# A two-layer decoder trunk on one core: where the seven-product sums are combined, which rings the short weight chunks use, and how far the up projection runs ahead

## The chip, the cores and the metric

One core of one Trainium2 chip. The metric is the device time of one execution in microseconds (us), the median of the runs shown. The engines are called by their names in the profile: PE (TensorE), DVE (VectorE), ACT (ScalarE), POOL (GpSimd), SP (SyncE, which issues the weight loads).

## The reference

The kernel computes two residual layers on x of 256 positions by 2048 channels, all in float32, and a last RMSNorm. Each layer has a mixer (attention of several kinds, with an input and an output projection) and an MLP:

```
for layer in range(DEPTH):                 # DEPTH = 2
    h = rms_norm(x, attn_norm[layer])
    x = x + mixer(h)                       # even: MLA and MoBA, odd: dilated and sliding window
    h = rms_norm(x, mlp_norm[layer])
    x = x + jnp.square(jax.nn.relu(h @ w_up[layer])) @ w_down[layer]
return rms_norm(x, final_norm)
```

`w_up[layer]` is 2048 x 8192 and `w_down[layer]` 8192 x 2048. The change touches the MLPs, the way in which all weights are split, and where the gain of the last norm is loaded.

## The kernel before, in words

**Numbers.** A product in float32 is made of three passes on PE: each operand is split into a `hi` and a `lo` half, and hi\*hi, hi\*lo and lo\*hi are summed in PSUM. ACT makes `hi` (line 1276, a copy that rounds), DVE makes `lo` (line 1284, the difference).

**Weights and the stream.** All weights come in units of up to 1 MB (tile `raw`, three buffers, loaded by SP) and are used in chunks of up to 1024 columns. One list, `stream`, has all chunks in the order in which PE uses them; the main loop walks it. Before chunk i it makes `hi` up to chunk i + 4 and `lo` up to chunk i + 3 (`hi_to(i + HI_BUFS)`, `lo_to(i + LO_BUFS)`, rings of 5 and 4 slots of 1024 columns). When the `lo` of a unit's last chunk is made, the unit's buffer is free, and the next unit's load is issued. Each engine executes its instructions in the order in which this loop writes them.

**The MLP.** The 8192 hidden channels are cut into eight groups of 1024. A group's up projection (`up_list`, kind "U", 16 chunks) gives `up` banks, and `up_done` applies relu and the square. Groups 0 to 6, the plain groups, go down by a scheme of seven products in place of eight (Strassen's, in Winograd's form): `product_list` has, for each of four column blocks `cb` of 512 output columns, eight chunks of kind "S"; one in four, `single`, is only 512 columns wide. DVE prepares the sums of weight blocks (`prep13`, `prep24`, tiles `w13` and `w24`). The seven products of a column block stand in the PSUM banks `s0` and `s1`; `products_done` copies them to `stage` (ACT) and adds them to `sums` in DRAM with an accumulating DMA of POOL (line 1077). In the stream two product chunks of group g stand before each up chunk of group g + 1. Group 7 goes down directly, at the end of the MLP (kind "T", and "last" for the last block of the second MLP): eight blocks of 256 output columns, two chunks each; `down_done` evacuates a block, scales it and adds it to `xT`.

**The combine.** In group 6, when a column block's second bank is done, `products_done` starts a job `combine(cb)`: it reads the sums of that column block from DRAM (line 1085, tile `s` of the ring `hs`), DVE adds the seven products to four results (lines 1090 to 1095), ACT scales them (line 1098), PE transposes them in two halves (line 1105), and DVE adds each half to `xT` (line 1106). When both the combine and the direct part of a block are done, `finish` starts what follows: in the first MLP `make_xs` (the next mixer's input, lines 233 and 234, and a sum of squares, 241 to 245), in the second `final_block` (transposes and products with the gain, line 1197), at the end `last_block`.

**Jobs.** A job is a Python generator that writes its next instructions at a tick; `yield d, pe` puts its next step d ticks later. There is a tick after each second product chunk, after each up chunk and after each chunk of the direct down projection. The main loop writes a chunk's matmuls first, then the tick's.

## Time and profile before

| what | value |
|---|---|
| median of three runs | 2223.31 us (2222.3 to 2231.39) |
| the profiled execution, its own time | 2223.32 us |
| its span, first to last instruction | 2221.5 us |
| mean granted clock of PE | 0.987 of 2.4 GHz |
| PE busy | 2156.0 us, 97% |
| PE weight loads busy | 2058.3 us, 93% |
| DVE busy | 1745.0 us, 79% |
| ACT busy | 1316.7 us, 59% |
| POOL busy | 108.9 us, 5% |
| moved by DMA | 455.51 MB, mean 205 GB/s |

The shares are means over stages. The page's slices show PE at nine tenths or more nearly everywhere, and less in a few slices near 1000 us and after 2050 us. A wait of PE counts there; idle time of another engine counts only if PE waits for it.

### The profile page before, as it was taken

What the parts mean: (1) busy time and instruction counts of PE and PEld (TensorE: products, weight loads), DVE (VectorE), ACT (ScalarE), POOL (GpSimd) and SP (SyncE); (2) the same over time, 40 slices, a digit from 0 to 9 for tenths busy, and PEclk for the clock granted to TensorE, in tenths of its full rate; (3) what the DMA queues carried; (4) which work ended last, traced back from release to release, by engine and by line L of the source; (5) the groups of instructions that cost most, each with busy time, mean ns of one, the idle gap of its engine ahead of it and who ended that gap; (6) DMA issues with size and microseconds to landing.
All of it is one profiled execution on the core that took longest, in us unless ns stands there. A gap on an engine that the chain in (4) does not pass through costs nothing.

```text
span 2221.5 us, 39419 instructions
## 1 busy us (share of the span) xinstructions
PE 2156.0 (97%) x16086; PEld 2058.3 (93%) x16086; DVE 1745.0 (79%) x2248; ACT 1316.7 (59%) x1777; POOL 108.9 (5%) x144
## 2 busy tenths in 40 slices
PE   9999999999999999978999999999999999999787
PEld 7898989999999999978888899899999999999776
DVE  6765666898999999977966665568898999999766
ACT  6554545566667666655655446455666666666553
POOL 0000000000000000000000000000000000000000
PEclk9999999999999999999999999999999999999898
DMA  8545456577888888877554456565778888888772
GB/s 264 171 148 161 152 188 177 183 248 216 239 229 246 232 240 240 238 218 227 175 171 136 154 185 191 147 191 179 250 223 241 229 242 235 240 239 233 210 230 83
DMA packets 297685, 455.51 MB, mean 205 GB/s; under 512 B 10696, under 2 KB 172560, under 8 KB 297376
## 3 DMA queue, kind: packets, MB, share of 16 engines
q1 hardware_dynamic: 280224, 392.32, 56.0%
q0 software_dynamic: 17248, 60.67, 13.0%
q8 instruction: 126, 2.06, 0.4%
q14 instruction: 55, 0.45, 0.1%
q10 hardware_dynamic: 32, 0.01, 0.0%
HBM read 399.49 MB, written 53.48 MB: 204 GB/s over the span
## 4 chain that ended last, share of the span: by engine, by line
issue 26%; PE 20%; DMA 2%; POOL 2%; DVE 2%; ACT 1%; POOLq 0%; ACTq 0%; DVEq 0%; SPq 0%
PE mm L472 7%; PE mm L473 4%; POOL sums L1077 2%; PE mm L457 1%; PE mm L458 1%; PE mm L459 1%; DMA sums<-stage 1%; DMA hs<-sums 1%; PE up L463 1%; PE up L464 1%; PE up L465 1%; DVE lo L1284 1%; PE side L350 1%; DMA raw<-w_up 1%; PE mm L475 1%
## 5 line engine op out<-in xcount | busy, mean ns | idle before, releaser
L1284 DVE TENSOR_TENSOR lo<-raw,hi 128x1024 fp32r<-128x1024 f32 (+1 forms) x756 | 825.1, 1113 | 189.2 <-PE mm L473 74.9
L1276 ACT ACTIVATE hi<-raw 128x1024 fp32r<-128x1024 f32 (+1 forms) x756 | 717.9, 966 | 413.8 <-DMA raw<-w_up 169.2
L465 PE MATMUL up<-xs,lo 128*128 128x256 f32 x2048 | 579.6, 283 | 6.6 <-DVE lo L1284 6.2
L463 PE MATMUL up<-xs,hi 128*128 128x256 f32 x2048 | 578.8, 283 | 1.6 <-DVE xT L757 1.6
L464 PE MATMUL up<-xs,hi 128*128 128x256 f32 x2048 | 579.0, 283 | 0.0
L496 PE MATMUL s<-hi,hs 128*128 128x256 f32 x1568 | 445.7, 284 | 0.0
L497 PE MATMUL s<-lo,hs 128*128 128x256 f32 x1568 | 444.1, 283 | 0.0
L498 PE MATMUL s<-hi,hs 128*128 128x256 f32 x1568 | 443.7, 283 | 0.0
L465 PEld LDWEIGHTS up<-xs,lo 128*128 128x128 f32 x2048 | 387.8, 189 | 12.0 <-DVE lo L1284 11.2
L463 PEld LDWEIGHTS up<-xs,hi 128*128 128x128 f32 x2048 | 385.2, 188 | 1.9 <-ACT hi L1276 1.9
L464 PEld LDWEIGHTS up<-xs,hi 128*128 128x128 f32 x2048 | 385.0, 188 | 0.0
L472 PE MATMUL mm<-xs,hi 128*128 128x512 f32 x885 | 319.5, 401 | 0.4 <-ACT hi L1276 0.4
L1276 ACT ACTIVATE hi<-w 128x1024 fp32r<-128x1024 f32 x224 | 236.1, 1054 | 130.3 <-DVE w L1050 85.6
L496 PEld LDWEIGHTS s<-hi,hs 128*128 128x128 f32 x1568 | 300.1, 191 | 0.0
L497 PEld LDWEIGHTS s<-lo,hs 128*128 128x128 f32 x1568 | 300.1, 191 | 0.0
L498 PEld LDWEIGHTS s<-hi,hs 128*128 128x128 f32 x1568 | 299.5, 191 | 0.0
L1284 DVE TENSOR_TENSOR lo<-w,hi 128x1024 fp32r<-128x1024 f32 x224 | 273.8, 1222 | 24.2 <-ACT hi L1276 18.9
L473 PE MATMUL mm<-xs,lo 128*128 128x256 f32 x944 | 259.3, 280 | 0.2 <-DVE lo L1284 0.2
L472 PEld LDWEIGHTS mm<-xs,hi 128*128 128x128 f32 x885 | 166.1, 188 | 38.1 <-ACT hi L1276 0.9
L473 PEld LDWEIGHTS mm<-xs,lo 128*128 128x128 f32 x944 | 177.5, 188 | 3.0 <-DVE lo L1284 0.5
L1043 DVE TENSOR_TENSOR w<-raw 128x1024 f32<-128x1024 f32 x112 | 136.4, 1218 | 0.0
L1077 POOL DMA_DIRECT2D sums<-stage x96 | 82.9, 863 | 973.0 <-ACT stage L1072 955.8
(302 smaller groups left out, 2669.9 us busy)
## 6 DMA issues: line engine op xcount, KB each, us to landing
raw<-w_up SPq DMA_DIRECT2D x128, 1024.0 KB, 5.8
raw<-w_down SPq DMA_DIRECT2D x128, 1024.0 KB, 6.4
raw<-od_w_in SPq DMA_DIRECT2D x36, 1024.0 KB, 5.0
raw<-ev_w_in SPq DMA_DIRECT2D x30, 1024.0 KB, 5.3
sums<-stage POOLq DMA_DIRECT2D x56, 512.0 KB, 6.1
sums<-stage POOLq DMA_DIRECT2D x56, 384.0 KB, 6.4
raw<-ev_w_out SPq DMA_DIRECT2D x16, 1024.0 KB, 5.0
raw<-od_w_in SPq DMA_DIRECT2D x20, 512.0 KB, 4.4
```

The source lines that it names most:

```text
L463: mm(ps[:, j], hi[:, n, c], m[:, 0:T], start=first and j == 0, stop=False)
L464: mm(ps[:, j], hi[:, n, c], m[:, T:], start=False, stop=False)
L465: mm(ps[:, j], lo[:, n, c], m[:, 0:T], start=False, stop=last and j == 1)
L472: mm(ps[:, j], hi[:, n, c], m, start=first, stop=False)
L473: mm(ps[:, j, 0:T], lo[:, n, c], m[:, 0:T], start=False, stop=False)
L496: mm(ps, x[:, a, 0:P], hi[:, o, q], start=first and at % 2 == 0, stop=False)
L497: mm(ps, x[:, a, 0:P], lo[:, o, q], start=False, stop=False)
L498: mm(ps, x[:, a, P:], hi[:, o, q], start=False, stop=last and (at % 2 == 1 or prod == 3))
L1043: tt(four(t), w[:, :, :, 1].rearrange("p q k c -> p k q c"), w[:, :, 0].rearrange("p q h c -> p h q c"), op=OP.subtract)
L1077: nc.gpsimd.dma_start(to, stage, accum_op=OP.add)
L1276: act(d, r, AF.Copy)
L1284: tt(d, r, f32(h), op=OP.subtract)
```

## The change

It has four parts, all in the MLPs or in the splitting of weights. (1) The four combines of an MLP are all started after the last column block of group 6, one tick apart, and their steps are spaced by 4 + cb, 2 and 1 ticks; so their reads stand behind the last accumulate, and their computing stands in the direct down projection of group 7. (2) The gain of the last norm, a tile of 8 KB a partition until now, is loaded at the same point into the buffers of `w13` and `w24`, in two halves. (3) The 512-wide chunks get rings of their own (`hi4` and `lo4`, two slots each); `split_ahead` makes `hi` and `lo` as far ahead as each ring has room. (4) 18 up chunks stand before the first products, where there were 16, so that the up chunk beside two product chunks is two further on; the last four product chunks have no up chunk beside them.

```diff
--- before.py
+++ after.py
@@ -118,8 +118,10 @@
 
 
 
-    def __init__(self, unit, kts, views, prep=None, prods=()):
+
+    def __init__(self, unit, kts, views, prep=None, prods=(), small=None):
         self.unit, self.kts, self.views, self.prep, self.prods = unit, kts, views, prep, prods
+        self.small = small
         unit.users += 1
 
 
@@ -973,9 +975,16 @@
         def open_pool():
             open_banks(pool_ctx, f"mlp{layer}_ps")
             E["pool"] = pool_ctx.enter_context(tc.tile_pool(name=f"mlp{layer}", bufs=1, reuse_waits="tile"))
-            if last:
-                fn = E["fn"] = E["pool"].tile([P, D], F32, name="fn")
-                nc.gpsimd.dma_start(fn, final_norm.unsqueeze(0).to_broadcast([P, D]))
+
+        def load_gain():
+            fn = [E["pool"].tile([P, D // 2], F32, name=n) for n in ("w13", "w24")]
+            for i in range(2):
+                c = slice(i * D // 2, (i + 1) * D // 2)
+                nc.gpsimd.dma_start(fn[i], final_norm[c].unsqueeze(0).to_broadcast([P, D // 2]))
+            E["fn"] = lambda c0, n: fn[c0 // (D // 2)][:, c0 % (D // 2):c0 % (D // 2) + n]
+
+        def small(name):
+            return E["pool"].tile([P, 512], F32R, name=name + "4", bufs=2)
 
         NGRP = 8
         W = FF // NGRP
@@ -1060,7 +1069,7 @@
 
                 ks = [a // 2, a // 2 + 1]
                 chunks += [Chunk(unit, ks, plain, prods=((X11, 1), (X12, 2))),
-                           Chunk(unit, ks, single, prods=((S4, 3),)),
+                           Chunk(unit, ks, single, prods=((S4, 3),), small=small),
                            Chunk(unit, ks, of(13), prep13, ((S1, 5), (S3, 7))),
                            Chunk(unit, ks, of(24), prep24, ((S2, 6), (X22, 4)))]
             return chunks
@@ -1075,15 +1084,18 @@
                     nc.gpsimd.dma_start(to, stage)
                 else:
                     nc.gpsimd.dma_start(to, stage, accum_op=OP.add)
-                if grp == NGRP - 2 and half == "s1":
-                    jobs.spawn(combine(cb), keys=[("sum", cb)], delay=1)
+                if grp == NGRP - 2 and half == "s1" and cb == 3:
+                    for i in range(4):
+                        jobs.spawn(combine(i), keys=[("sum", i)], delay=i)
+                    if last:
+                        load_gain()
             return f
 
         def combine(cb):
 
             s = E["pool"].tile([P, 7, 2 * P], F32, name="hs", bufs=2 * nb)
             nc.gpsimd.dma_start(s, sums[cb].rearrange("p (o c) -> p o c", o=7))
-            yield 3, 0
+            yield 4 + cb, 0
             p1, p2, p3, p5, p7, p6, p4 = (s[:, i] for i in range(7))
             g = E["pool"].tile([P, 2, 2, T], F32, name="hr", bufs=1)
             u2, u43 = temp(), temp()
@@ -1096,7 +1108,7 @@
             r = E.setdefault("r", st["r"])
             for tok in range(2):
                 act(g[:, tok], g[:, tok], AF.Copy, scale=r[:, tok:tok + 1])
-            yield 1, 1
+            yield 2, 1
             for i in range(2):
                 b = 2 * cb + i
                 ps = side().rearrange("p (j t) -> p j t", j=2)
@@ -1159,11 +1171,12 @@
                       for cb in range(4)]
             return [(block, i) for block in blocks for i in range(len(block.chunks))]
 
-        stream.extend(up_list(0))
-        for grp in range(NGRP - 1):
-            s, u = product_list(grp), up_list(grp + 1)
-            for i in range(len(u)):
-                stream.extend(s[2 * i:2 * i + 2] + u[i:i + 1])
+        ups = [c for grp in range(NGRP) for c in up_list(grp)]
+        prods = [c for grp in range(NGRP - 1) for c in product_list(grp)]
+        lead = KT // 4 * nb + 2
+        stream.extend(ups[:lead])
+        for i in range(len(prods) // 2):
+            stream.extend(prods[2 * i:2 * i + 2] + ups[lead + i:lead + i + 1])
 
         def h_mov(kt):
             need(("h", layer, NGRP - 1, kt // 2))
@@ -1193,7 +1206,7 @@
             for tok in range(2):
                 for j in range(2):
                     nc.tensor.transpose(pv[:, tok, j * P:(j + 1) * P], xT[b][:, j, tok * P:(tok + 1) * P], ident)
-            fn = E["fn"][:, b * T:(b + 1) * T]
+            fn = E["fn"](b * T, T)
             tt(st["o"][:, :, b * T:(b + 1) * T], pv, fn[:, None, :].to_broadcast([P, 2, T]), op=OP.mult)
         jobs.spawn(job())
         jobs.step(jobs.jobs[-1])
@@ -1218,7 +1231,7 @@
                 nc.tensor.transpose(turn[:, j * T + tok * P:j * T + (tok + 1) * P], xl[:, j, tok * P:(tok + 1) * P], ident)
             c0 = 7 * T + j * P
             tt(o[:, :, c0:c0 + P], turn[:, j * T:(j + 1) * T].rearrange("p (t c) -> p t c", c=P),
-               E["fn"][:, None, c0:c0 + P].to_broadcast([P, 2, P]), op=OP.mult)
+               E["fn"](c0, P)[:, None].to_broadcast([P, 2, P]), op=OP.mult)
 
         add_up(acc[:, 0], True, False)
         turn_out(0)
@@ -1265,11 +1278,25 @@
         chunk = block.chunks[c]
         return chunk.views(chunk.unit.raw, dst)
 
+
+    held = {"hi": [0, 0], "lo": [0, 0]}
+    bufs = {"hi": (HI_BUFS, 2), "lo": (LO_BUFS, 2)}
+
+    def take_half(kind, i):
+        chunk = stream[i][0].chunks[stream[i][1]]
+        held[kind][chunk.small is not None] += 1
+        return chunk.small(kind) if chunk.small else wts.tile([P, 1024], F32R, name=kind, bufs=bufs[kind][0])
+
+    def room(kind):
+        i = at[kind]
+        small = i < total and stream[i][0].chunks[stream[i][1]].small is not None
+        return i < total and held[kind][small] < bufs[kind][small]
+
     def hi_to(n):
         while at["hi"] < min(n, total):
             i = at["hi"]
-            his[i] = wts.tile([P, 1024], F32R, name="hi", bufs=HI_BUFS)
             prep = stream[i][0].chunks[stream[i][1]].prep
+            his[i] = take_half("hi", i)
             if prep:
                 prep()
             for d, r in views(i, his[i]):
@@ -1279,7 +1306,7 @@
     def lo_to(n):
         while at["lo"] < min(n, total):
             i = at["lo"]
-            los[i] = wts.tile([P, 1024], F32R, name="lo", bufs=LO_BUFS)
+            los[i] = take_half("lo", i)
             for (d, r), (h, _) in zip(views(i, los[i]), views(i, his[i])):
                 tt(d, r, f32(h), op=OP.subtract)
             at["lo"] += 1
@@ -1293,8 +1320,17 @@
         hi_to(n)
         lo_to(n)
 
+    def split_ahead():
+        while room("hi"):
+            hi_to(at["hi"] + 1)
+        while room("lo") and at["lo"] < at["hi"]:
+            lo_to(at["lo"] + 1)
+
     def chunk(i):
         block, c = stream[i]
+        small = block.chunks[c].small is not None
+        for kind in held:
+            held[kind][small] -= 1
         consume(block, c, his.pop(i), los.pop(i))
 
 
@@ -1382,8 +1418,7 @@
         if i in starts:
             phases[starts[i] - 1][2]()
             phases[starts[i]][1]()
-        hi_to(i + HI_BUFS)
-        lo_to(i + LO_BUFS)
+        split_ahead()
         chunk(i)
         block, c = stream[i]
         if block.tiles * len(block.chunks[c].kts) == 8 or block.kind == "S" and c % 2:
```

### How the rows move

POOL's queue at the end of the first MLP's group 6 (`sums_0` to `sums_3` are the four column blocks' sums in DRAM). Before:

```order
L1077 DMA sums_0_98<-stage 128x1024
L1085 DMA hs<-sums_0_98 128x1792
L1077 DMA sums_1_99<-stage 128x768
L1077 DMA sums_1_99<-stage 128x1024
L1085 DMA hs<-sums_1_99 128x1792
L1077 DMA sums_2_100<-stage 128x768
L1077 DMA sums_2_100<-stage 128x1024
L1085 DMA hs<-sums_2_100 128x1792
L1077 DMA sums_3_101<-stage 128x768
L1077 DMA sums_3_101<-stage 128x1024
L1085 DMA hs<-sums_3_101 128x1792
```

and now:

```order
L1086 DMA sums_2_100<-stage 128x768
L1086 DMA sums_2_100<-stage 128x1024
L1086 DMA sums_3_101<-stage 128x768
L1086 DMA sums_3_101<-stage 128x1024
L1097 DMA hs<-sums_0_98 128x1792
L1097 DMA hs<-sums_1_99 128x1792
L1097 DMA hs<-sums_2_100 128x1792
L1097 DMA hs<-sums_3_101 128x1792
```

A read stood right behind the accumulate that it has to wait for; now all four stand behind the last one, and only the fourth reads what was written just ahead.

DVE, first combine of the first MLP. Before, in the plain group (L1284 is a `lo`, L1043 to L1050 prepare sums of weight blocks, L1106 adds to the residual xT):

```order
L1284 TENSOR_TENSOR lo<-raw,hi 128x512
L1090 TENSOR_TENSOR t<-hs 128x256
L1091 TENSOR_TENSOR hr<-hs 128x256
L1092 TENSOR_TENSOR t<-t,hs 128x512
L1093 TENSOR_TENSOR hr<-t,hs 128x256
L1094 TENSOR_TENSOR hr<-t,hs 128x256
L1095 TENSOR_TENSOR hr<-t,hs 128x256
L1043 TENSOR_TENSOR w_10810<-raw 128x1024
L1284 TENSOR_TENSOR lo<-raw,hi 128x1024
L1106 TENSOR_TENSOR xT_89<-xT_89,side 128x512
```

and now, in the direct down projection (L1311 is a `lo`, L1140 to L1143 evacuate a block, L1118 adds to xT):

```order
L1143 TENSOR_TENSOR xT_90<-xT_90,t 128x512
L1102 TENSOR_TENSOR t<-hs 128x256
L1103 TENSOR_TENSOR hr<-hs 128x256
L1104 TENSOR_TENSOR t<-t,hs 128x512
L1105 TENSOR_TENSOR hr<-t,hs 128x256
L1106 TENSOR_TENSOR hr<-t,hs 128x256
L1107 TENSOR_TENSOR hr<-t,hs 128x256
L1311 TENSOR_TENSOR lo<-raw,hi 128x1024 x2
L1140 TENSOR_TENSOR t<-s_11607,t 128x512
L1142 TENSOR_TENSOR t<-t,rB 128x512
L1143 TENSOR_TENSOR xT_91<-xT_91,t 128x512
L1118 TENSOR_TENSOR xT_89<-xT_89,side 128x512
```

The six operations and the two additions to xT of three combines have moved from between product chunks to between the blocks of the direct down projection, where the fourth already was.

ACT in the same direct down projection. Before, with one combine in it (L1276 is a `hi`, L1127 evacuates a block, L1098 scales a combine, L233 to L244 make the next mixer's input):

```order
L1276 ACTIVATE hi<-raw 128x1024
L1127 ACTIVATE t<-s_11566 128x512
L1276 ACTIVATE hi<-raw 128x1024
L1098 ACTIVATE hr<-hr,r 128x512 x2
L233 ACTIVATE xs<-xT_89,gT 128x256 x2
L241 ACTIVATE acc<-xT_89 128x512
L1276 ACTIVATE hi<-raw 128x1024
L1127 ACTIVATE t<-s_11618 128x512
```

and now (L1303 is a `hi`, L1139 evacuates, L1110 scales, L235 to L246 make the input):

```order
L1303 ACTIVATE hi<-raw 128x1024 x2
L1139 ACTIVATE t<-s_11672 128x512
L1110 ACTIVATE hr<-hr,r 128x512 x2
L235 ACTIVATE xs<-xT_89,gT 128x256 x2
L243 ACTIVATE acc<-xT_89 128x512
L235 ACTIVATE xs<-xT_90,gT 128x256 x2
L246 ACTIVATE t<-xT_90 128x512
L1303 ACTIVATE hi<-raw 128x1024 x2
```

The scalings of all four combines now stand here, and the input of two blocks at a time follows a combine, ahead of the next two `hi`.

## Rows read from the trace of the kernel before

**Rows 1.** The page, section 1: busy us, share of the span, instructions.

```profile
PE 2156.0 (97%) x16086; PEld 2058.3 (93%) x16086; DVE 1745.0 (79%) x2248; ACT 1316.7 (59%) x1777; POOL 108.9 (5%) x144
```

**Rows 2.** Waits of PE: for whom, total us, times, longest us.

```profile
PE side L1105 <- ACT hr L1098: 43.1, 9, 7.6
PE up L465 <- DVE lo L1284: 6.2, 13, 1.6
```

**Rows 3.** Windows: length, busy us of each engine, PEclk, DMA share, GB/s.

```profile
545.00:552.00 7.00, 5.41 (x45) 5.21 (x45) 5.78 (x7) 4.08 (x5) 0.00 (x0) 1.00 0.79 241
850.00:950.00 100.00, 99.94 (x836) 99.58 (x835) 92.23 (x106) 66.59 (x78) 7.76 (x9) 1.00 0.83 235
958.00:1042.00 84.00, 67.73 (x513) 66.35 (x512) 60.90 (x75) 42.91 (x50) 6.84 (x9) 0.90 0.69 206
1042.00:1053.80 11.80, 11.77 (x69) 10.03 (x67) 6.26 (x7) 5.26 (x7) 0.57 (x1) 1.00 1.04 311
1064.00:1100.00 36.00, 36.00 (x209) 31.44 (x208) 35.59 (x52) 22.19 (x35) 2.01 (x6) 1.00 0.57 175
2066.00:2152.00 86.00, 67.23 (x515) 65.72 (x515) 60.64 (x74) 42.91 (x50) 6.80 (x9) 0.88 0.68 202
2175.00:2208.00 33.00, 33.00 (x214) 29.65 (x213) 26.90 (x36) 12.47 (x18) 0.00 (x0) 1.00 0.20 65
```

**Rows 4.** Timeline of the first combine: start us, us, instruction, [idle before it].

```profile
951.98 0.86 POOL L1077 DMA_DIRECT2D sums<-stage  x1 [3.94 <-ACT stage L1072]
958.76 0.57 POOL L1085 DMA_DIRECT2D hs<-sums  x1 [5.92 <-PE s L498]
...
966.46 0.42 DVE L1090 TENSOR_TENSOR t<-hs 128x256 f32<-128x256 f32 x1 [6.66 <-DMA hs<-sums]
...
969.04 1.33 ACT L1098 ACTIVATE hr<-hr,r 128x512 f32<-128x512 f32 x2 [6.14 <-DVE hr L1095]
...
969.82 1.52 PE L1105 MATMUL side<-misc,hr 128*128 128x128 f32 x4 [6.84 <-ACT hr L1098]
```

**Rows 5.** Windows of the eight stretches at half clock: the first, and their sum.

```profile
969.80:974.55 4.75, 4.59 (x21) 4.30 (x21) 4.54 (x6) 2.59 (x4) 0.00 (x0) 0.50 0.03 6
...
sum 35.01, PE 33.94 PEld 30.93 DVE 30.57 ACT 20.93 POOL 0.00; mean PE 4.24 PEld 3.87 DVE 3.82 ACT 2.62 POOL 0.00
```

**Rows 6.** Timeline of DVE, one block of the first direct down projection.

```profile
1084.56 1.22 DVE L1284 TENSOR_TENSOR lo<-raw,hi 128x1024 fp32r<-128x1024 f32 x1
1085.69 0.69 DVE L1128 TENSOR_TENSOR t<-s,t 128x512 f32<-128x512 f32 x1
...
1088.88 0.87 DVE L234 SCALAR_TENSOR_TENSOR xs<-xT,gT,xs 128x256 fp32r<-128x256 f32 x2
1089.67 0.68 DVE L245 TENSOR_TENSOR acc<-acc,t 128x512 f32<-128x512 f32 x1
1090.28 1.22 DVE L1284 TENSOR_TENSOR lo<-raw,hi 128x1024 fp32r<-128x1024 f32 x1
```

**Rows 7.** Timeline of DVE, the fourth combine: first and last of six operations.

```profile
1054.92 0.42 DVE L1090 TENSOR_TENSOR t<-hs 128x256 f32<-128x256 f32 x1 [2.82 <-DMA hs<-sums]
...
1056.99 0.42 DVE L1095 TENSOR_TENSOR hr<-t,hs 128x256 f32<-128x256 f32 x1
```

**Rows 8.** Timeline: start and end of the two direct down projections.

```profile
1042.38 0.40 PE L472 MATMUL s<-hs,hi 128*128 128x512 f32 x1
...
1101.72 0.88 DVE L234 SCALAR_TENSOR_TENSOR xs<-xT,gT,xs 128x256 fp32r<-128x256 f32 x2 [1.24 <-ACT xs L233]
...
2151.95 0.39 PE L472 MATMUL s<-hs,hi 128*128 128x512 f32 x1
...
2208.99 0.41 DVE L1207 TENSOR_TENSOR t<-up,rB 128x256 f32<-128x256 f32 x1
```

**Rows 9.** Lines of ACT, 1040 to 1110 us: busy us, mean ns, idle before.

```profile
L1276 ACT ACTIVATE hi<-raw 128x1024 fp32r<-128x1024 f32 x17 | 17.8, 1050 | 2.1 <-DMA raw<-od_w_in 2.1
...
L1098 ACT ACTIVATE hr<-hr,r 128x512 f32<-128x512 f32 x2 | 1.3, 714 | 7.8 <-DVE hr L1095 7.8
```

## The prediction, made before the changed kernel had run

> **What bounds the kernel now.** I read the page's busy times first: TensorE (PE) is busy 97% of the span [rows 1], so only a stretch where it waits or runs slowly can give time back. Its list of waits comes next: 43.1 us in nine waits belong to one line, the transposes L1105 of a combine, which wait for ScalarE's scaling L1098; 6.2 us in 13 waits are for a `lo` half that is late [rows 2]. The windows show the price per stretch. In the plain group of 850 to 950 PE issues 836 matmuls in 100 us at clock 1.00; in 958 to 1042, where three combines stand, 513 in 84 us at mean clock 0.90; in 2066 to 2152, the same place of the second MLP, 515 in 86 us at 0.88 [rows 3]. The timeline shows one such wait: GpSimd issues the last accumulate of a column block at 951.98, can issue the read of the same sums only at 958.76, the data reach VectorE at 966.46, which adds for 2.4 us, ScalarE scales at 969.04, and the transposes start at 969.82 after 6.84 us of idle PE [rows 4]. Then the granted clock is 0.50, the lower level of 1.2 GHz, until 974.55: PE, idle just before, pays twice. There are eight such places (four column blocks, two MLPs), and their slow stretches sum to 35.0 us, of which half is lost [rows 5].
>
> I call the last group's down projection the tail (16 chunks T0 to T15 of four row tiles, two to an output block of 256 columns). There VectorE is the second bound: in 1064 to 1100 it is busy 35.59 of 36 us [rows 3], and one block is 5.72 us of back-to-back work, from `lo` at 1084.56 to `lo` at 1090.28 [rows 6]. PE needs about the same, 2.86 us a chunk.
>
> **The change, part by part.**
>
> *Combines taken out of the plain group.* All four reads move behind the last accumulate, and VectorE's and ScalarE's parts go into the tail. What goes: at 8.36 matmuls a us [rows 3] the 513 need 61.4 us of the 84, the 515 need 61.6 of the 86, so 22.6 and 24.4 us are lost there now, 47.0 together. (Cross-check: six eighths of 43.1 us of waits, plus half of six eighths of 35.0 us at half clock, is 45.) VectorE and ScalarE are not late there otherwise: 92.2 and 66.6 us busy of 100 in the plain group [rows 3]. Term: **-47.0**.
>
> *Reads.* Four reads stand behind each other on GpSimd's queue, and in the second MLP two gain loads ahead of them; an issue takes 0.57 us [rows 4]. Three of the four read sums that landed long before. The first is wanted by VectorE only after T3 and the second block's addition, about 14 us after T0, and a read took 966.46 - 958.76 = 7.7 us [rows 4]. Cover is therefore some 6 us; the DMA engines are full there (share 1.04 at 311 GB/s in 1042 to 1053.8 [rows 3]) and get 2.75 MB more. Without that cover the wait of before returns in the tail (third rival). Taken at 0. The gain's load leaves the start of the second MLP, where nobody waits for it.
>
> *Combines put into the tail.* VectorE gets three more there: each 2.4 us of six operations (1054.92 to the end of the last near 1057.4 [rows 7]) and two additions to xT, of the size of L245's 0.61. In the tail of the first MLP its order now holds, from the first block's evacuation (6.5 us after T0: two chunks and ScalarE's copy) to the last xs of block 7: 15 `lo` of 1.13, eight evacuations of 2.06, four combines of 2.4, eight xT additions of 0.61, eight xs pairs of 0.79 and seven sums of squares of 0.61 [rows 6, 7]: 17.0 + 16.5 + 9.6 + 4.9 + 6.3 + 4.3 = 58.6 us, so with about 1.2 us of waiting for T2 and T3 it ends 66 us after T0. Before, the same point is 1102.6 - 1042.4 = 60.2 after T0 [rows 8], its own wait and slow clock included: +5.5, a little rounded down. Two chains come on top. In program order the transposes of combine k stand right behind chunk T(5 + 2k), and VectorE, now late, ends its part after that; PE then waits for 1 to 2 us, since ScalarE's two scalings (0.71 each) come in between [rows 9]. And ScalarE's queue puts those scalings and two xs blocks between two `hi` copies of 1.05 [rows 9], so a `lo` behind them waits too. I take 1 us for each combine: +4, so **+9.5**; bounds 0 (the mixer behind the tail makes it up) and +14 (2 us a link).
>
> In the second MLP the same list, without xs but with seven output products of 0.61 and without the chunks behind T15, is 12.4 + 14.4 + 9.6 + 4.9 + 4.3 + 4.0 = 49.6 us: 57.3 after T0, where the last block's first operation stands now at 2208.99 - 2151.95 = 57.0 [rows 8]. VectorE has room there, 26.9 us busy of 33 [rows 3]. So only the chains count: **+4.5**, bounds -1 and +9.
>
> *Clock.* PE's new waits in the tails are shorter than the old. The nearest rows: the eight waits of the combines each brought 0.50, 35.0 / 8 = 4.4 us of it, 2.2 us lost [rows 5]; the stretch 545 to 552, with the longest wait for `lo`, 1.6 us, stayed at 1.00 [rows 2, 3]. The last combine's wait is likely the longest, 3 to 4 us; I take one drop per tail, half of it hidden since VectorE is the late one: **+2.2** in both, bounds 0 and 8.8 (two drops each, none hidden). The Trainium skill (TensorE: Matmul & The Clock Gate, "A second HAM failure mode: psum-queue depth-cycling") says that frequent micro-idles between groups of matmuls can also make the clock swing between its levels. By that rule the tails would pay the upper bound; the row with a single short wait speaks against it, but no row here has a series of them, so it stands as a rival.
>
> *Rings for the short chunks.* The four big `hi` and `lo` slots no longer hold the 512-wide chunk, so both run about one chunk further ahead. The operations are the same. What it can save is the 6.2 us of waits for `lo` [rows 2]; bounds 0 and -6.2, taken near the upper since a chunk ahead (12 or 24 matmuls, 1.4 to 2.9 us at 8.36 a us) is about the longest of them or more: **-4.5**.
>
> *Up projection two chunks ahead.* No wait of PE for `hs` is in its list [rows 2]; it only fills the order differently. The last four product chunks of a layer then run without up chunks between them, where VectorE needs about a us more than PE; the `lo` ring covers that. 0.
>
> Sum: -47.0 + 9.5 + 4.5 + 2.2 - 4.5 = -35.3. The profiled execution took 2223.3 us (span 2221.5), as the median of the runs, 2223.3: **2188 us**, range of this case alone 2178 to 2199.
>
> **Rivals.**
>
> *The tails take the combines for nothing.* For it: before, VectorE idles 5.5 of the 11.8 us from 1042 on [rows 3]. Against it: it waits there for the first blocks, which it still must. -47.0 - 4.5: 2172 us.
>
> *The tails take them badly.* Each link costs 2 us and the clock falls twice in a tail: -47.0 - 3 + 14 + 9 + 8.8 gives 2205 us. For it: VectorE has no idle left in the first tail, and both it and ScalarE execute in order.
>
> *The change doesn't do what it says.* The reads land late one behind the other on full DMA engines, and six combines wait in the tail as before, at (43.1 + 17.5) / 8 = 7.6 us each with the clock: -47.0 - 4.5 + 45.6, about 2217 us. Against it: the cover above, growing with each combine. The Trainium skill (DMA: Bandwidth & Descriptors, "Queues, rings and completion order") says that each DMA engine takes turns between its queues packet by packet, which would slow the weight loads as well as the reads; no row here shows the two queues apart.
>
> *Slower than before.* The place is every plain group: `hi` copies further ahead stand in ScalarE's queue before the evacuations of the product banks. If a load's wait so delays the bank of the next column block, there are 56 column blocks; at the longest wait of now, 1.6 us, that is 90 us: 2278 us. It decides from 35.3 / 56 = 0.63 us each. Against it: the order of loads is the same, and `lo`, which frees their buffers, runs ahead too.
>
> **How the numbers follow.** Forecast 0.50; nothing paid in the tails 0.20; badly paid 0.19; waits moved 0.06; slower 0.05. About 0.5% (11 us) is what a measurement of this kernel can tell from no change: the first three are faster, 0.89; moved waits are the same, 0.06; slower 0.05. The range 2170 to 2208 takes in the forecast and most of the two cases beside it, and leaves out about a fifth.
>
> **What would show it.** Right: L1105's counterpart has no long wait between the product groups, whose last group runs at 8.3 or more matmuls a us at clock 1.00; VectorE is near fully busy in the first 60 us of the first tail, PE waits there several times for 1 to 4 us, and the tail is some 10 us longer than now; waits for `lo` in the groups fall below 2 us. Wrong: transposes that wait for a read's landing (third rival), a clock of 0.50 over much of the tails (second), or new waits of PE for product banks in the groups (fourth).

## The result, and the profile after

| | before | after |
|---|---|---|
| median | 2225.91 us (4 runs, 2222.3 to 2231.39) | 2434.70 us (4 runs, 2433.61 to 2435.19) |
| ratio after to before | | 1.0935, 95% interval 1.0909 to 1.0961 |
| profiled execution | 2223.32 us | 2433.61 us |
| mean granted clock | 0.987 | 0.969 |

The change made the kernel 209 us **slower**. The prediction said 2188 us and gave slower a chance of 0.05. It was wrong, and by far more than any of its bounds.

The page of the changed kernel, section 1 (busy us, share of the span, instructions), answers to [rows 1]:

```profile
PE 2237.4 (92%) x16086; PEld 2106.2 (87%) x16086; DVE 1743.3 (72%) x2248; ACT 1313.7 (54%) x1777; POOL 109.2 (4%) x145
```

DVE and ACT do the same work as before, to 3 us. Of PE's 81 us more, some 46 are the lower clock, by an estimate (0.031 of 2432 us lost, where it was 0.013 of 2222); the rest was not taken apart. So nothing was added: every engine is idle more. The windows (columns as in [rows 3]) tell where:

```profile
850.00:950.00 100.00, 86.82 (x676) 84.01 (x675) 72.35 (x85) 54.48 (x65) 5.66 (x7) 0.97 0.69 191
...
1800.00:1900.00 100.00, 87.89 (x667) 85.26 (x666) 72.78 (x85) 54.48 (x65) 6.03 (x7) 0.93 0.71 191
```

The stretch 850 to 950 is the plain group of [rows 3], which had 836 matmuls, DVE busy 92.23 us, clock 1.00. It is not the place of the combines; it is a part for which the prediction had no term but the -4.5 of the rings. Counted in windows of 50 us, 500 to 1100 holds 4122 matmuls and 1750 to 2350 holds 4114. At the 418 per window of before they need 493 and 492 us in place of 600 each, so against that pace 215 us are lost there. That is not yet the balance, since the kernel before lost 47.0 us to its combines in these groups. From an MLP's first `up` matmul to the first matmul of its tail, the direct down projection, it took 681.2 and 681.6 us before (361.15 to 1042.38, 1470.35 to 2151.95) and takes 767.9 and 764.8 after (361.16 to 1129.07, 1577.66 to 2342.41): 170 us more. The other 40 us lie behind these marks, where the combines are now.

The waits of PE after (for whom, total us, times, longest), against [rows 2]:

```profile
PE up L465 <- ACT hi L1303: 69.9, 42, 2.6
PE up L467 <- DVE lo L1311: 47.8, 87, 0.8
PE s L499 <- DVE lo L1311: 26.6, 25, 1.4
PE side L1117 <- ACT hr L1110: 15.6, 9, 3.8
...
PE s L474 <- ACT stage L1081: 4.1, 2, 2.1
```

The 43.1 us of waits for a combine's scaling did go (15.6 are left, in the tails). In their place stand 144 us of waits for `hi` and `lo` of weight chunks. One step up, the waits of ACT and of DVE in the changed kernel (one answer each, its first line):

```profile
ACT hi L1303 <- DMA raw<-w_up: 307.2, 52, 7.7
...
DVE lo L1311 <- ACT hi L1303: 280.4, 120, 5.9
```

The same two lines of the kernel before. The first, in its total, stood in the page from which I predicted, and I made no use of it; the second I had not read:

```profile
ACT hi L1276 <- DMA raw<-w_up: 169.2, 80, 5.5
...
DVE lo L1284 <- ACT hi L1276: 45.1, 140, 1.8
```

So PE waits for `lo`, DVE for `hi`, ACT for the landing of a `w_up` load. What the load waits for is in the timeline: SP issues it when `prep24` (L1058, L1059) has read the buffer that it goes into, since there are three `raw` buffers. (For a unit of product weights it is this, and not the `lo` of the last chunk, that frees the buffer: that `lo` reads `w24`.) First the kernel before, one column block (start us, us, engine, instruction):

```profile
857.71 0.37 SPq L1141 DMA_DIRECT2D raw<-w_up  x1
...
865.49 0.86 POOL L1077 DMA_DIRECT2D sums<-stage  x1 [3.87 <-ACT stage L1072]
866.94 0.37 SPq L1141 DMA_DIRECT2D raw<-w_up  x1
...
869.41 0.28 DVE L1011 TENSOR_TENSOR hr<-hr 128x128 f32<-128x128 f32 x1
...
874.66 1.06 ACT L1276 ACTIVATE hi<-raw 128x1024 fp32r<-128x1024 f32 x1 [1.71 <-DMA raw<-w_up]
...
878.38 0.69 DVE L1050 TENSOR_TENSOR w<-raw,w 128x512 f32<-128x512 f32 x1
879.14 0.37 SPq L1141 DMA_DIRECT2D raw<-w_up  x1
```

Then the changed kernel, one column block:

```profile
863.25 0.37 SPq L1153 DMA_DIRECT2D raw<-w_up  x1
...
867.63 0.29 DVE L1020 TENSOR_TENSOR hr<-hr 128x128 f32<-128x128 f32 x1
...
875.47 0.69 DVE L1059 TENSOR_TENSOR w<-raw,w 128x512 f32<-128x512 f32 x1
876.05 0.86 POOL L1086 DMA_DIRECT2D sums<-stage  x1 [6.28 <-ACT stage L1081]
876.22 0.37 SPq L1153 DMA_DIRECT2D raw<-w_up  x1
...
887.10 1.06 ACT L1303 ACTIVATE hi<-raw 128x1024 fp32r<-128x1024 f32 x1 [7.43 <-DMA raw<-w_up]
888.19 1.23 DVE L1311 TENSOR_TENSOR lo<-raw,hi 128x1024 fp32r<-128x1024 f32 x1 [5.66 <-ACT hi L1303]
888.21 0.39 PE L465 MATMUL up<-xs,hi 128*128 128x256 f32 x1 [2.60 <-ACT hi L1303]
...
890.05 0.69 DVE L1059 TENSOR_TENSOR w<-raw,w 128x512 f32<-128x512 f32 x1
890.80 0.37 SPq L1153 DMA_DIRECT2D raw<-w_up  x1
```

This is a loop, two turns to a column block: `prep24` ends, the load is issued, it lands, ACT makes `hi`, DVE makes `lo`, and in DVE's order the next `prep24` stands behind that `lo`. Before, the turns are 9.23 and 12.20 us (857.71 to 866.94 to 879.14), 21.4 together, which is PE's own time for a column block, 180 matmuls (84 of products and 96 of the up projection) at 8.40 a us, the pace of the runs below in which PE does not wait in these groups. After, they are 12.97 and 14.58 (863.25 to 876.22 to 890.80): 27.55 us. Two long things lie in a turn: the preparation of the moving operand (L1011 or L1020 and what follows, the "hs job") and a load that is issued close to a 512 KB accumulate. Before, one turn has both and they overlap; the other has neither. After, one turn has the hs job and the other the slow load, so both count. The DMA views of the two kernels show the slow load's time (last column: us from issue to landing). The changed kernel, 876 to 879:

```profile
raw<-w_up SPq DMA_DIRECT2D x1, 1024.0 KB, 10.8
sums<-stage POOLq DMA_DIRECT2D x1, 512.0 KB, 10.4
```

and the kernel before, 866 to 869:

```profile
raw<-w_up SPq DMA_DIRECT2D x1, 1024.0 KB, 7.6
sums<-stage POOLq DMA_DIRECT2D x1, 512.0 KB, 6.1
```

In the other turns the load takes 5.4 us (before, 857.71, with a 384 KB accumulate issued 3.05 us behind it) and 5.7 (after, 863.25, with one 5.67 us behind it).

These are single loads. Between 600 and 905 us the slow load takes 7.6 to 8.8 us before, and 9.6 to 10.8 after, so that 876.22 is the longest. Ten column blocks of the changed kernel, from its load at 612.24 to this one, take 26.4 us each.

The same stretch shows what sets a turn. In the changed kernel every turn without the hs job lasts as long as its load takes to land, plus 3.8 us (`hi`, `lo` and the two operations of `prep24`): 13.4 to 14.6 us, but for one. There the load was issued just ahead of the accumulate, by 0.11 us, where it is 0.17 us behind it in all others:

```profile
719.45 0.37 SPq L1153 DMA_DIRECT2D raw<-w_up  x1
719.56 0.86 POOL L1086 DMA_DIRECT2D sums<-stage  x1 [6.55 <-ACT stage L1081]
...
730.52 0.37 SPq L1153 DMA_DIRECT2D raw<-w_up  x1
```

The view of 719 to 721 has the load:

```profile
raw<-w_up SPq DMA_DIRECT2D x1, 1024.0 KB, 7.2
```

The turn took 11.07 us. The turns with the hs job last 12.96 or 12.97 us, whatever their load took. Before, the turns without the job are landing plus 3.8 to 4.0 us as well (9.2 to 9.6), those with it 12.1 to 12.6, the longest of them a landing of 8.8 plus 3.8. So the kernel before stood at the limit of the same loop already.

### The profile page after: what moved, and what is told of

Read it like the earlier page. It is cut to its first block, busy times and chain, and to the rows that moved or that the text cites. A ratio compares the mean times of both kernels' runs of the same rounds, so it can differ in the third digit from the quotient of the medians.

```text
span 2431.8 us, 39167 instructions
## 1 busy us (share of the span) xinstructions
PE 2237.4 (92%) x16086; PEld 2106.2 (87%) x16086; DVE 1743.3 (72%) x2248; ACT 1313.7 (54%) x1777; POOL 109.2 (4%) x145
## 4 chain that ended last, share of the span: by engine, by line
PE 38%; issue 31%; DVE 12%; DMA 11%; ACT 5%; POOL 2%; ACTq 0%; POOLq 0%; DVEq 0%; SPq 0%
PE mm L474 13%; DMA raw<-w_up 9%; PE mm L475 7%; DVE lo L1311 6%; ACT hi L1303 3%; PE up L467 2%; PE up L465 2%; PE up L466 2%; PE mm L459 2%; PE mm L461 2%; PE mm L460 2%; POOL sums L1086 2%; DVE w L1052 1%; DVE w L1059 1%; DVE w L1058 1%
## 5 line engine op out<-in xcount | busy, mean ns | idle before, releaser
L1311 DVE TENSOR_TENSOR lo<-raw,hi 128x1024 fp32r<-128x1024 f32 (+1 forms) x756 | 824.4, 1112 | 441.8 <-ACT hi L1303 279.3
L1303 ACT ACTIVATE hi<-raw 128x1024 fp32r<-128x1024 f32 (+1 forms) x756 | 703.9, 963 | 529.4 <-DMA raw<-w_up 307.2
L465 PE MATMUL up<-xs,hi 128*128 128x256 f32 x2048 | 599.8, 293 | 71.5 <-ACT hi L1303 69.9
L467 PE MATMUL up<-xs,lo 128*128 128x256 f32 x2048 | 607.1, 296 | 47.9 <-DVE lo L1311 47.8
L466 PE MATMUL up<-xs,hi 128*128 128x256 f32 x2048 | 596.0, 291 | 0.0
L465 PEld LDWEIGHTS up<-xs,hi 128*128 128x128 f32 x2048 | 404.5, 198 | 80.5 <-ACT hi L1303 80.5
L467 PEld LDWEIGHTS up<-xs,lo 128*128 128x128 f32 x2048 | 406.1, 198 | 68.4 <-DVE lo L1311 66.2
L466 PEld LDWEIGHTS up<-xs,hi 128*128 128x128 f32 x2048 | 404.2, 197 | 0.0
L1303 ACT ACTIVATE hi<-w 128x1024 fp32r<-128x1024 f32 x224 | 236.6, 1056 | 298.4 <-DVE w L1052 170.9
L1311 DVE TENSOR_TENSOR lo<-w,hi 128x1024 fp32r<-128x1024 f32 x224 | 273.1, 1221 | 4.5 <-ACT hi L1303 0.3
```

The source lines that it names most:

```text
L465: mm(ps[:, j], hi[:, n, c], m[:, 0:T], start=first and j == 0, stop=False)
L466: mm(ps[:, j], hi[:, n, c], m[:, T:], start=False, stop=False)
L467: mm(ps[:, j], lo[:, n, c], m[:, 0:T], start=False, stop=last and j == 1)
L1303: act(d, r, AF.Copy)
L1311: tt(d, r, f32(h), op=OP.subtract)
```

## The experiments

Fourteen kernels, each in one run unless a ratio is given. "C" is the late combine, "R" the rings for the short chunks, "L" the lead of 18. The gain's load is late in all of them. In the first four expectations the theories have their own numbers; from e5 on theory 1 is the load loop.

### The parts alone and in pairs (e1 to e5, e9)

e1, C alone, against the changed kernel (the short chunks also lose `small`):

```diff
-        lead = KT // 4 * nb + 2
+        lead = KT // 4 * nb + 0
...
-        split_ahead()
+        hi_to(i + HI_BUFS)
+        lo_to(i + LO_BUFS)
```

> Only the late combines and the late gain; rings as before, no extra up chunks ahead. The slow stretch of the change is the plain groups (26 us a column block where 21.4 were), which this part does not touch: every theory expects the plain groups at the pace of before (836 matmuls in 100 us) and no combine waits in the last of them. By the sum of the prediction without its ring term, 2192 us (bounds 2175 to 2210). If the combines were the cause of the slow plain groups, it would be near 2435.

e2, R alone (with the first hunk of e1), and e3, L alone (with its second), have the combines put back:

```diff
-                if grp == NGRP - 2 and half == "s1" and cb == 3:
-                    for i in range(4):
-                        jobs.spawn(combine(i), keys=[("sum", i)], delay=i)
+                if grp == NGRP - 2 and half == "s1":
+                    jobs.spawn(combine(cb), keys=[("sum", cb)], delay=1)
...
-            yield 4 + cb, 0
+            yield 3, 0
...
-            yield 2, 1
+            yield 1, 1
```

> Only the rings for the short chunks (with the late gain load, which makes room for them); combines as before, no extra up chunks ahead. Theory 1, the deeper rings are the cause: about 2223 + (2435 - 2188) = 2470 us, with PE waits for hi of the up chunks. Theory 2, the two up chunks ahead are the cause: 2217 to 2223 us. Theory 3, only both together: 2217 to 2223 us.

> Only the two up chunks ahead; rings and combines as before. Theory 1, the rings: 2223 us. Theory 2, the up chunks ahead: about 2470 us, with PE waits for hi of the up chunks. Theory 3, only both together: 2223 us.

e4 is C and L (second hunk of e1), e5 is C and R (first hunk of e1), e9 is R and L (the combines put back, nothing else):

> The change without its rings. Theory 1, the rings: about 2190 us, as with the late combines alone. Theory 2, the up chunks ahead: about 2435 us, as the whole change. Theory 3, only both together: about 2190 us.

> The changed kernel with 16 up chunks ahead, as before, in place of 18: combines and rings are new, the lead is not. With e1 to e4 and the changed kernel it makes the table of parts complete. Theory 1 (load loop: with three raw buffers each w_up load is issued when the prep24 before it ends; rings and lead each shift the loop's place against the accumulates and the hs job, and only both together close it into one chain): about as e4, 2250 to 2290 us, the plain groups at 785 to 810 matmuls in 100 us. Theory 2 (the rings alone put hi copies ahead of work that ACT and DVE owe to PE, once the combines no longer give the groups a pause): nearly as slow as the changed kernel, over 2380 us, groups under 750 matmuls in 100 us.

> The changed kernel with the combines put back into the last plain group (spaced as before; the gain is loaded after the last of them): rings and lead alone. It is the last cell of the table of parts. If the excess of the changed kernel comes from rings and lead meeting in the load loop, it is there without the late combines too: 2400 us or more, groups under 750 matmuls in 100 us. If the late combines are one of the three that it takes, the parts add up: 2227 + 51 + 64, about 2340 us, groups near 770.

Measured, with the kernel before from the same runs, and the matmuls in 850 to 950 us:

| | us | less before | matmuls in 100 us |
|---|---|---|---|
| before | 2224.1 to 2228.0 | | 836 |
| C (e1) | 2213.2, ratio 0.9943 (0.9927 to 0.9960) | -13.1 | 833 |
| R (e2) | 2277.2 | +51.0 | 815 |
| L (e3) | 2290.6 | +64.3 | 804 |
| C and L (e4) | 2257.5 | +31.2 | 801 |
| C and R (e5) | 2259.7 | +31.7 | 799 |
| R and L (e9) | 2471.1 | +247.0 | 688 |
| all three | 2434.7 | +208.8 | 676 |

R and L alone add up to 115 us, together they cost 247: 132 more. With C in all cells the same sum is 44.8 + 44.3 = 89 against 221.9, again 133 more. So the excess belongs to the pair R and L, and C has no part in it; C makes every row faster, by 13 to 38 us. The expectations that one part alone would carry the loss fell, and so did the third, that neither costs anything by itself. C alone is 21 us above the 2192 expected of it and outside its bounds; e8, below, shows that loads hold it up too.

### The loads (e6)

```diff
-                else:
+                elif grp == NGRP - 2:
                     nc.gpsimd.dma_start(to, stage, accum_op=OP.add)
```

> The changed kernel without the accumulating DMAs of groups 1 to 5 of both MLPs (the sums then hold groups 0 and 6 alone; stage is still written, and nothing else is left out). It leaves every queue of PE, DVE, ACT and SP as in the changed kernel, and takes 2 x 5 x 8 transfers away that meet the w_up loads. Theory 1a (a w_up load that is issued together with an accumulate lands 3 to 4 us later, and that makes the loop longer than PE's 21.4 us a column block): groups back to over 815 matmuls in 100 us, 2200 to 2270 us. Theory 1b (the loop is too long by the order of the engines' queues, hs job and preparation between lo and hi, whatever the load takes): groups under 750 matmuls in 100 us, 2380 us or more; between the two, both have a part.

2274.1 us, 160.6 less than the changed kernel, with not one instruction of PE, DVE or ACT taken out. Its window 850 to 950 and ACT's wait for the load:

```profile
850.00:950.00 100.00, 98.17 (x811) 96.75 (x812) 89.00 (x104) 64.92 (x75) 0.00 (x0) 1.00 0.59 190
```

```profile
ACT hi L1303 <- DMA raw<-w_up: 153.1, 55, 6.9
```

SP issues the `w_up` loads at 860.49, 873.47 and 882.89, turns of 12.98 and 9.42 us, and the load of the second turn takes 5.6 us. The turn with the hs job is as long as in the changed kernel (12.97); the other is again the landing plus 3.8 us, and shorter by 4.0 to 5.2 than the 13.4 to 14.6 of there. The answer lies between 1a and 1b, nearer to 1a: some three quarters of the loss go with the accumulates, and the loop without them is still longer than PE's time (22.4 us against 21.4). The share is rough, since the kernel before was not run without them.

### A fourth buffer (e7, e8, e10, e13, e14)

If the loop is right, a fourth `raw` buffer opens it: the load goes into a buffer that was free long before, and its landing is off the chain. The 8 KB come from the gain's tile. The core of the edit, beside a rule in the loader that takes this buffer for one unit at a time when the three are taken:

```diff
+        def spare():
+            if "pool" in E:
+                return E["pool"].tile([P, 2048], F32, name="rawx", bufs=1)
```

e7 is e4 with it, e8 is e1 with it, e10 has it alone (C, R and L as before):

> e4 (late combines and a lead of 18 up chunks, old rings) with a fourth raw buffer in the MLPs, out of the 8 KB that the gain's tile no longer takes. Theory 1 (the loop from prep24 over the load's issue and landing to hi, lo and the next prep24): with four buffers a load is issued half a column block earlier, so its landing is no longer waited for; groups over 820 matmuls in 100 us, waits of PE for lo under 10 us, 2195 to 2225 us against 2257.5 for e4. Rival (the order in ACT's and DVE's queues alone costs the time): no better than 2250.

> e1 (late combines alone) with a fourth raw buffer in the MLPs. Theory 1: e1's 9.6 us of waits for lo, and its stretches under 825 matmuls in 100 us, come from the same loop, so they go: 2195 to 2208 us, ratio to before 0.986 to 0.992. Rival (what e1 loses against the forecast lies in the tails, where no load is late): 2211 to 2216 us, ratio 0.993 to 0.996, as e1.

> Combines, rings and lead as before; only the gain is loaded late, and its 8 KB are a fourth raw buffer in the MLPs. What the late combines are worth where no load is late is then this run less e8 (2189.9). By the terms of my prediction, -47.0 + 9.5 + 4.5 + 2.2 = -31: about 2221 us, with the waits for the combine's transposes near 43 us still there. If the late combines were worth only what e1 showed, 13 us: about 2203.

| | without | with a fourth buffer |
|---|---|---|
| C, R, L as before | 2224.1 | 2216.1 (e10) |
| C | 2213.2 (e1) | 2189.9 (e8), ratio to before 0.9833 (0.9817 to 0.9850) |
| C and L | 2257.5 (e4) | 2193.2 (e7) |

The lead costs 44 us with three buffers and 3 with four. All three runs have 840 matmuls in 850 to 950, at clock 1.00, the full rate of PE. e8 is faster than both kernels, by 38 us against before, and better than I expected of it: C is worth 26.3 us (2216.1 - 2189.9; some 30 with each set against its own runs of before) where no load is late, and showed only 13 where one is.

For all parts there was no room, until the short rings had one slot each and the two `stage` tiles their own sizes, which frees 5 KB. That is e13, the control. DVE, PE and SP have the changed kernel's order in it; ACT's, against the expectation, differs: one short `hi` of a column block stands two instructions later (54 times in all).

```diff
-            return E["pool"].tile([P, 512], F32R, name=name + "4", bufs=2)
+            return E["pool"].tile([P, 512], F32R, name=name + "4", bufs=1)
...
-                stage = E["pool"].tile([P, 4 * T], F32, name="stage", bufs=2)[:, 0:n * T]
+                stage = E["pool"].tile([P, n * T], F32, name="stage%d" % n, bufs=1)
...
-    bufs = {"hi": (HI_BUFS, 2), "lo": (LO_BUFS, 2)}
+    bufs = {"hi": (HI_BUFS, 1), "lo": (LO_BUFS, 1)}
```

> The changed kernel with one slot in place of two in each short ring (hi4, lo4), and the stage of the two banks of a column block as one tile each of its own size. ACT, DVE and SP execute the same instructions in the same order as in the changed kernel; it frees 5 KB, so that e14 has room. Both theories: within 1.5% of the changed kernel, 2400 to 2470 us, groups at 660 to 720 matmuls in 100 us. If it came out under 2350, the second slots would themselves be what costs.

> e13 with a fourth raw buffer in the MLPs: all three parts of the change (late combines, rings of 5 + 1 and 4 + 1 slots with hi one chunk ahead of lo, lead of 18). Theory 1 (the load of w_up is what the loop waits for): groups at 835 to 841 matmuls in 100 us, no wait of ACT for raw<-w_up over 100 us, 2186 to 2200 us. Rival (the order in ACT's and DVE's queues that rings and lead make together costs the time, whatever the loads do): groups under 800, over 2250 us, with DVE waiting for hi in the groups while no load is late.

e13: 2434.3 us, the changed kernel's time. e14, the same with the fourth buffer: **2199.3 us**, ratio to before 0.9886 (0.9869 to 0.9902), 235 us less than its control. One window of e14, and the first of ACT's waits, with no load among the seven longest:

```profile
850.00:950.00 100.00, 99.42 (x827) 98.60 (x828) 91.10 (x105) 67.57 (x80) 7.76 (x9) 1.00 0.84 236
```

```profile
ACT hi L1328 <- DVE w L1057: 199.6, 90, 2.6
ACT hi L1328 <- DVE w L1064: 105.0, 110, 2.5
```

The loads are still slow: the page's median of a 512 KB accumulate is 8.7 us in e14 (9.4 in the changed kernel, 6.1 before), and the `w_up` load issued at 854.83 took 8.8 us. ACT waits for none of them now. The timeline of SP in e14:

```profile
842.90 0.37 SPq L1158 DMA_DIRECT2D raw<-w_up  x1
...
854.83 0.37 SPq L1158 DMA_DIRECT2D raw<-w_up  x1
...
864.70 0.37 SPq L1158 DMA_DIRECT2D raw<-w_up  x1
```

Its two turns, 11.93 and 9.87 us, sum to 21.8, near PE's own 21.4, and they stay at that length between 600 and 905 us, with landings from 6.3 to 9.6 us. That settles the main question: the loss was the wait for the loads, not the order in which the change queues work on ACT and DVE, which is the same in e13 and e14. What is left beside e8, 827 matmuls in place of 840 (835 to 841 were expected) and 9.4 us, may be that order; no run shows it.

### Shorter hi rings (e11, e12)

My first way to make room was another one, and it misled me:

```diff
-    bufs = {"hi": (HI_BUFS, 2), "lo": (LO_BUFS, 2)}
+    bufs = {"hi": (HI_BUFS, 1), "lo": (LO_BUFS, 2)}
...
-RAW_BUFS, HI_BUFS, LO_BUFS = 3, 5, 4
+RAW_BUFS, HI_BUFS, LO_BUFS = 3, 4, 4
```

(`hi4` also has one slot.) e12 has the fourth buffer beside it.

> The changed kernel with hi rings of 4 and 1 slots in place of 5 and 2, so that hi runs no further ahead than before, and lo as in the change. If hi's lead over lo is what closes the loop (hi of the next units takes ACT and waits there for a load in front of the work that DVE waits for), about e4: 2250 to 2300 us. If lo's greater lead does it (DVE then makes lo and the preparation in a bunch), it stays over 2380 us.

> e11 with a fourth raw buffer in the MLPs (the shorter hi rings make the room): all parts of the change, with the load issued half a column block earlier. Theory 1 (loads): groups at 835 to 841 matmuls in 100 us, 2186 to 2198 us, as e7 and e8. Rival (rings and lead cost time by the order in the queues, whatever the loads do): over 2215 us.

2521.9 us, and 2418.2 with the fourth buffer (ratio 1.0874, 1.0855 to 1.0894). e11 lies in the range of its second expectation (over 2380), though for neither reason, and e12 by itself would have spoken against the loads. But its waits are others. DVE's first, and its timeline:

```profile
DVE lo L1336 <- ACT hi L1328: 488.2, 395, 4.1
```

```profile
864.45 1.22 DVE L1057 TENSOR_TENSOR w<-raw 128x1024 f32<-128x1024 f32 x1
866.87 1.23 DVE L1336 TENSOR_TENSOR lo<-w,hi 128x1024 fp32r<-128x1024 f32 x1 [1.21 <-ACT hi L1328]
...
868.74 0.69 DVE L1064 TENSOR_TENSOR w<-raw,w 128x512 f32<-128x512 f32 x1
870.55 1.23 DVE L1336 TENSOR_TENSOR lo<-w,hi 128x1024 fp32r<-128x1024 f32 x1 [1.13 <-ACT hi L1328]
```

With `hi` and `lo` rings of the same length both run equally far ahead, so a sum (L1057) is followed on DVE by its own `lo`, and DVE waits while ACT makes the `hi` between them: 395 waits of some 1.2 us. No load is among ACT's seven longest waits here. In e14, where `hi` is one slot longer than `lo`, the `lo` of another chunk stands between, and DVE waits for `hi` 58.8 us in 71 waits. So e12 was a bad test of the loads; it measured the price of the rings. The kernels e12 and e14 differ by one slot of `hi` and one of the short `lo` ring, and no run has one without the other.

## Why the prediction was wrong

**The step that failed** is the pair "*Rings for the short chunks* ... The operations are the same" (-4.5, bounds 0 and -6.2) and "*Up projection two chunks ahead.* No wait of PE for `hs` is in its list [rows 2]; it only fills the order differently. ... 0." Both were costed from PE's list of waits alone, and neither had a bound on the loss side. Measured alone they cost 51 and 64 us, together 247. What I left out was in the profile before: DVE busy 92.23 of 100 us [rows 3], which leaves a loop through DVE little to spare; ACT waiting 169.2 us for `w_up` loads, behind which `lo` and the next preparation stand; and the load's issue, tied to the end of a preparation on DVE. PE hardly waited because the slow load and the hs job happened to lie in the same turn of that loop. Both edits move exactly such things against each other. That no operation was added was true and proved nothing.

**The fourth rival** had the right place (every plain group) and sign, and the wrong mechanism. It let `hi` copies delay the evacuation of product banks; PE's wait for `stage` is 4.1 us in all, both times at the start of a tail (1129.07 and 2342.41), and its 2278 us fell short by 157. Its argument against itself, "the order of loads is the same", is what misled: the order is, the times of issue are not.

**The third rival** (reads late) did not come true in the tails: DVE waits there once for a read, 2.5 us. But what it took from the Trainium skill (DMA: Bandwidth & Descriptors, "Queues, rings and completion order"), that a DMA engine takes turns between its queues packet by packet, I set aside because no row showed the two queues apart. Rows for it were there to be asked for: in the kernel before, 5.3 to 5.8 us for one `w_up` load of a column block and 7.6 to 8.8 for the other, with an accumulate issued 1.4 to 1.6 us ahead of it. So the loads are slowed, as such turns would have it, though no row shows the turns themselves; e6 and e14 show the price.

**Combines out of the plain group, and into the tail.** Where no load is late, e10 and e8 differ by C alone. Their windows from the first matmul of the tail to the last `xs` (first MLP), and to the first operation of the last block (second MLP), the marks of [rows 8]. e10:

```profile
1037.90:1098.11 60.21, 54.67 (x301) 47.28 (x300) 49.11 (x72) 34.46 (x54) 2.57 (x7) 0.94 0.57 171
2141.02:2201.39 60.37, 52.74 (x314) 46.50 (x312) 42.03 (x58) 22.79 (x31) 1.15 (x3) 0.92 0.34 110
```

and e8:

```profile
1009.12:1082.68 73.56, 61.68 (x333) 52.63 (x332) 60.25 (x95) 37.56 (x60) 3.67 (x10) 0.93 0.56 183
2099.63:2175.15 75.52, 59.66 (x338) 51.59 (x336) 52.90 (x82) 26.11 (x37) 2.71 (x6) 0.91 0.36 128
```

| term | forecast | measured, e8 less e10 |
|---|---|---|
| combines out of the plain groups | -47.0 | -54.7: the first tail starts 28.8 earlier, and from its end to the second one it is 26.0 less |
| first tail | +9.5 (0 to +14) | +13.4 |
| second tail | +4.5 (-1 to +9) | +15.2 |
| clock in the tails | +2.2 (0 to 8.8) | inside the two rows above; 0.94 and 0.92 fell to 0.93 and 0.91, by an estimate 3.5 us more lost (8.4 in e10, 11.9 in e8) |
| sum | -30.8 | -26.2 (the times: 2189.9 - 2216.1 = -26.3) |

The mechanism was right, and the sum close; the second tail was mis-sized. DVE does have room there (52.90 of 75.52 us), as I said, but I priced the chains at 1 us for each combine, and they come to more. PE's waits in the second tail of e8:

```profile
PE side L1122 <- DVE xT L1123: 5.7, 2, 4.8
PE side L1214 <- DVE xs L1216: 5.6, 1, 5.6
PE side L1122 <- ACT hr L1115: 3.2, 4, 2.1
PE side L1214 <- DVE xT L1123: 1.0, 1, 1.0
```

15.5 us, against 7.2 in one wait in e10's. The long ones are not for ACT's scaling, which I had in view, but for a `side` bank that DVE has not yet read: transposes of combines and of finished blocks share these banks, and DVE takes them in its own order.

**The range** failed by its construction: all rivals but one were about the combines, the part of the change that had its row in PE's waits. The rings had the fourth, at 0.05 and outside the range; the lead had none.

What stays open: R alone was not run with a fourth buffer. Its own trace (e2, 600 to 905 us) shows the same loop, turns without the hs job of landing plus 3.8 us and turns with it of 12.95 us, or landing plus 3.8 where that is longer; but how much of its 51 us a buffer would give back is not shown. What sets the length of a turn with the hs job (12.2 us mostly before, 12.95 with R alone, 11.93 with L alone) and the 9.4 us between e14 and e8 were not taken apart.

## What to carry to other kernels

An edit that adds no operation and only changes how far ahead work is queued is not free where loads go into few buffers: follow the loop from a buffer's last reader to the load's issue, its landing, the work on it and the next last reader, and compare its length with the time that the bounding engine takes for the same work. Read for that the waits of the engines off the critical path, with the DMA behind them; that the bounding engine does not wait says nothing on how much slack the loop has. If it is within some per cent of being closed, give it a buffer first (here the 8 KB that another part of the change had freed) and reorder afterwards; and give every part of a change its own rival on the loss side, also the parts that seem to do nothing.

## What the runs showed of the hardware

Between 600 and 905 us a weight load of 1 MB took 5.3 to 6.3 us with no accumulates about (e6), 7.6 to 8.8 with a 512 KB accumulate issued 1.4 to 1.6 us ahead of it (before), and 9.6 to 10.8 with one issued 0.17 us ahead of it (changed kernel; another load follows 3.5 us behind, as it does in e6). It took 7.2 the one time that the load was issued 0.11 us ahead of the accumulate, which then took 10.0. The accumulate's median went from 6.1 to 9.4 us as well, at a mean of only 187 GB/s over the span. I had looked at the DMA engines' share only where they were full. The clock followed: beside the 42 waits of PE for `hi`, 2.6 us the longest, stand stretches at 0.50 (1.2 GHz) in the middle of the plain groups, 25 of them in 500 to 1100 and 1750 to 2350 us, 99 us together. The window right behind one such wait, in the changed kernel:

```profile
890.00:893.50 3.50, 3.50 (x20) 3.50 (x20) 3.07 (x4) 2.61 (x4) 0.00 (x0) 0.56 0.40 96
```

That it did not set the time, since the loop and not PE was the late one there, is argued and not shown; with the loads off the chain (e14) the plain groups stand at 1.00 again.
